# Row loads, spread rows, a lane for lambda and a split last store in a two-layer encoder

## The chip, the cores and the metric

The kernel runs on one core of one Trainium2 chip. The metric is the device time of one execution in microseconds, as the median of several runs. A core has five engines that take their instructions in order, each from its own queue: TensorE (PE, matrix products), VectorE (DVE), ScalarE (ACT), GpSimd (POOL) and SyncE (SP, which here issues nearly all DMAs). They wait for each other by semaphores. SBUF is the on-chip memory of 128 partitions, PSUM the banks that TensorE writes.

## The reference

Two layers of a bidirectional encoder on 256 tokens of width 2048. A layer norm opens it; each layer projects to six parts, runs a diagonal state space model on two of them and a difference of two softmax maps on four, projects back, and normalises again.

```python
x = layer_norm(x, ln_emb_g, ln_emb_b)
for l in range(DEPTH):
    proj = jnp.einsum('bsd,de->bse', x, w_in[l])
    u, g_ssm, q, k, v, g_attn = jnp.split(proj, PROJ_SPLITS, axis=-1)
    ...
    lam = (jnp.exp(jnp.sum(lambda_q1[l].astype(f32) * lambda_k1[l].astype(f32)))
           - jnp.exp(jnp.sum(lambda_q2[l].astype(f32) * lambda_k2[l].astype(f32)))
           + lambda_init)
    o = diff_attention(qh, kh, vh, lam)
    o = rms_norm(o, attn_norm_g[l]) * (1.0 - lambda_init)
    ...
    out = jnp.einsum('bse,ed->bsd', mix, w_out[l])
    x = layer_norm(DEEPNORM_ALPHA * x + out, ln_g[l], ln_b[l])
```

`layer_norm` takes mean and variance over the 2048 columns of a token, and then multiplies by a row g and adds a row b, the same for all tokens.

## The kernel before

**Weights.** They stream in as jobs of 512 KB. SP loads each into one of four `raw` buffers (L150). ScalarE rounds it to `wh` (L163), VectorE takes the rest `wl` = raw - wh (L165), and a product is three matmuls: wh with xh, wh with xl, wl with xh (L169 to L171). The activations are split in the same way into `xh` and `xl`. So TensorE can't go on without a cast on ScalarE and a subtraction on VectorE for each job.

**The layer norm.** x lies in the tile `H` as two blocks of 128 tokens. `ln_stats` (L202) takes the statistics of 256 columns, `bn_aggr` (L222) joins them, GpSimd adds eps (L224) and takes the power -1/2 (L225), giving `rstd`. Then for each piece of up to 512 columns VectorE runs a centre row (L230: minus mean, times g) and a scale row (L236: times rstd, plus b). TensorE transposes the result (L249), ScalarE copies it to `xh` (L253), VectorE makes `xl` (L254). Each finished piece is also stored to `xres` (L211, one DMA a piece, issued by SP from a lane). Behind the second layer the pieces go to `out` instead (L241): for the second block in `LAST_PIECES` of (6,5,5) tiles of 128 columns, with two stores a piece, one for each half of 64 partitions.

**g and b.** `load_gb` (L198, L199) loads a part of the row into all 128 partitions; 512 columns are 256 KB of DMA. Ahead of layer 0 four such pairs stand on SP between the loads of x, the first part of the constants `cst` (L800), the first raws and the rest of the constants (L806, called cst2 below).

**Lambda.** `lam_of` (L653 to L666) loads four rows `on`, multiplies them (L655), reduces (L657), takes the exponent `le`, joins them to `nlam` (L663), loads `gsc` (L665) and scales it (L666). It is called at the start of each layer. gsc has two buffers, so the one of layer 1 is loaded in the head already.

**Tables.** `ssm_tables` makes the state space tables on VectorE from `kx`, scaled by `p_st` = exp(`p_ls`) (L303 to L312, on through L350); TensorE transposes them (`tp`, L375).

**What sets the order.** The side work is written as generators in lanes, which are called between the matmul groups; what they issue goes to a scheduler that orders each engine's queue when the kernel is built. DMA issues use semaphores in turn, so an issue on SP also waits for the landing of the DMA that stands eight places ahead of it.

Of the kernel before, what the change touches and what calls it, by code (L numbers as in the profile page):

```python
# [21 lines left out]
EPS = 1e-5  # L22
# [6 lines left out]

C_ID, C_SEL, C_EYE, C_MF, C_MB, C_COS, C_SIN, C_HP, C_W = 0, 128, 192, 208, 209, 210, 466, 722, 723  # L30

LAST_PIECES = (6,5,5)
RAW_BUFS = 4
SPLIT_AHEAD = 2
BUDGET = 1.6
# [1 line left out]
STORE_HOP = 2  # L37
LOAD_HOP = 10
SCAN_COST = 1.0
HEAD_HOPS = (1,1,2,2,2,3)  # L40


@with_exitstack
def kernel(
# [29 lines left out]
    mult, add, sub = ALU.mult, ALU.add, ALU.subtract  # L74
# [140 lines left out]
    def ln_finish(r, gt, bt, st, dst, box, ahead):  # L215
# [4 lines left out]
        def moments(i):  # L220
            mv = T([128, 2], "mv", 2)
            V.bn_aggr(mv, st[:, i].rearrange("p c s -> p (c s)"))  # L222
            rstd = T([128, 1], "rstd", 2)
            GP.tensor_scalar(rstd, mv[:, 1:2], EPS, None, add)  # L224
            pool[0] = GP.tensor_tensor(rstd, rstd, mhalf[:, 0:1], ALU.pow).ins  # L225
            return mv, rstd

# [4 lines left out]
        def norm(i, k0, nk, mv, rstd):  # L232
            cs = slice(k0 * 128, (k0 + nk) * 128)
            if dst is None or i == 0:
                centre(i, k0, nk, mv)
            last = V.scalar_tensor_tensor(r[:, i, cs], r[:, i, cs], rstd, bt[:, cs], mult, add)  # L236
            if dst is None:
                stores.append((xres[128 * i:128 * i + 128, cs], r[:, i, cs]))
            else:
                for j in range(2):  # L240
                    SY.dma_start(dst[2 * i + j][:, cs], r[64 * j:64 * j + 64, i, cs])  # L241
            return last.ins

        def trans(k0, nk, i0, ni):
# [402 lines left out]

    swap = list(range(8, 16)) + list(range(0, 8)) + list(range(16, 32))

    def lam_of(l):  # L650
        t = T([128, 4, 64], "on")
        for i, src in enumerate((lambda_q1, lambda_k1, lambda_q2, lambda_k2)):
            SY.dma_start(t[:, i, :], src[l:l + 1, :].to_broadcast([128, 64]))  # L653
        tv = t.rearrange("p (m k) d -> p m k d", m=2)
        V.tensor_tensor(tv[:, :, 0, :], tv[:, :, 0, :], tv[:, :, 1, :], mult)  # L655
        s2 = T([128, 2], "ls2", 2)
        V.tensor_reduce(s2, tv[:, :, 0, :], AX.X, add)  # L657
        e2 = T([128, 2], "le2", 2)
        A.activation(e2, s2, AF.Exp)
        neg = T([128, 1], "nlam", 2)  # L660
        init = 0.8 - 0.6 * math.exp(-0.3 * l)

        V.scalar_tensor_tensor(neg, e2[:, 1:2], -init, e2[:, 0:1], add, sub)  # L663
        gs = T([128, 1], "gsc", 2)
        SY.dma_start(gs, attn_norm_g[l].unsqueeze(1))  # L665
        V.tensor_scalar(gs, gs, 1.0 - init, None, mult)  # L666
        return neg, gs

    def rotary(ps, scale):
        qs = T([128, 2, 256], "qs")  # L670
# [120 lines left out]


    r, gt, bt = ln_tiles()
    for i in range(2):
        for c in range(2):
            cs = slice(1024 * c, 1024 * c + 1024)
            for j in range(2):
                SY.dma_start(r[64 * j:64 * j + 64, i, cs], xv[2 * i + j][:, cs])
        if i == 0:
            SY.dma_start(cst[:, 0:C_SEL], consts[:, 0:C_SEL])  # L800
            load_gb(gt, bt, ln_emb_g, ln_emb_b, slice(0, 512))
    for c in range(RAW_BUFS):
        load(c)
        if c < 3:
            load_gb(gt, bt, ln_emb_g, ln_emb_b, slice(512 * c + 512, 512 * c + 1024))
    SY.dma_start(cst[:, C_SEL:], consts[:, C_SEL:])  # L806
    st = T([128, 2, 8, 6], "st")
    box = {}
# [48 lines left out]
    for l in range(DEPTH):  # L857
# [17 lines left out]
            z.ublocks = b + 1  # L875

        l_store = Lane(store_x(), 1.5)
        neg, gsc = lam_of(l)
        hi, lo = X.hi, X.lo
        acc2 = [acc_bank(), acc_bank()]  # L880
        for s in range(4):
# [15 lines left out]
        for hp in range(4):  # L897
# [11 lines left out]
            A.copy(v, acc)  # L909
            finish(rk)  # L910
            if hp == 0:
                l_out = Lane(ssm_out(l), 4, after=[l_scan])
            every += [Lane(head(hp, h, store["q"], store["k"], v, oT, neg, gsc), 1 + 0.1 * h) for h in range(2)]
            heads = every[-2:]
        for b in range(4):
            acc = block(hi, lo)
# [153 lines left out]
```

## Time and profile before

| | us |
|---|---|
| median of 3 runs | 1031.38 (1029.9 to 1032.72) |
| the profiled execution | 1032.34 |
| its span on the core | 1030.6 |
| TensorE busy | 965.9 |
| VectorE busy | 773.8 |
| ScalarE busy | 605.9 |
| GpSimd busy | 67.7 |

The granted clock of TensorE is 0.985 of full speed in the mean over the span. The span is divided here into a head (0 to 60 us: layer norm of x, first jobs, tables), layer 0, the switch between the layers (around 524 to 550), layer 1, and the tail (from 1010, behind the last matmul).

### The profile page before, as it was taken

Reading aid. Unit: us, or ns where it says so; the run is one execution under the profiler, and the core shown is the slowest. Engines: PE = TensorE matmul, PEld = TensorE weight load, DVE = VectorE, ACT = ScalarE, POOL = GpSimd, SP = SyncE. Lnnn points to the kernel's source line nnn. Section 1 sums busy time; section 2 is a strip of 40 time slices with the busy share of each in tenths; the row PEclk is TensorE's granted clock in tenths of the full one; section 3 lists DMA queues with packets and bytes.
Section 4 is the critical chain, followed back from the end, with each engine's and each line's share of the span. In section 5 each row is a group of like instructions: output and inputs, shape, how many; then the busy total and the mean of one; then the engine's idle time right before and its main releaser. Section 6 shows DMA issues by size and latency. Waiting matters only on the chain.

```text
span 1030.6 us, 23623 instructions
## 1 busy us (share of the span) xinstructions
PE 965.9 (94%) x9792; PEld 932.7 (91%) x9792; DVE 773.8 (75%) x1310; ACT 605.9 (59%) x962; POOL 67.7 (7%) x104
## 2 busy tenths in 40 slices
PE   2899999999999988999889999999999998999995
PEld 2889988999999887999879989999999897999995
DVE  6875799899887666655588699988988566565676
ACT  2546586655575899444344585565566879843640
POOL 1000131010010000000010120010010000000001
PEclk9999999999999998999999999999999999999998
DMA  9897522455465524779965724545455443677973
GB/s 270 240 271 218 179 62 62 146 182 165 144 193 164 174 88 124 247 241 303 275 207 166 232 59 146 177 152 162 152 162 179 142 144 104 179 231 238 316 241 85
DMA packets 201867, 186.08 MB, mean 181 GB/s; under 512 B 38048, under 2 KB 194464, under 8 KB 201760
## 3 DMA queue, kind: packets, MB, share of 16 engines
q1 hardware_dynamic: 201760, 184.57, 58.4%
q8 instruction: 77, 1.26, 0.5%
q14 instruction: 30, 0.25, 0.1%
HBM read 169.21 MB, written 15.34 MB: 179 GB/s over the span
## 4 chain that ended last, share of the span: by engine, by line
PE 66%; ACT 11%; DMA 9%; DVE 7%; issue 3%; SPq 3%; POOL 1%; POOLq 0%; DVEq 0%; ACTq 0%
PE acc L169 19%; PE acc L170 18%; PE acc L171 18%; DMA raw<-in_w_out_dram 3%; ACT bh L630 3%; DVE wl L165 2%; ACT bh L629 2%; DMA rpart<-xr 2%; ACT wh L163 2%; PE ss L502 2%; PE sc L699 1%; PE tp L474 1%; PE ss L727 1%; PE ss L592 1%; DVE H L236 1%
## 5 line engine op out<-in xcount | busy, mean ns | idle before, releaser
L165 DVE TENSOR_TENSOR wl<-raw,wh 128x1024 fp32r<-128x1024 f32 x266 | 324.7, 1222 | 182.2 <-ACT wh L163 181.2
L163 ACT CAST wh<-raw 128x1024 fp32r<-128x1024 f32 x266 | 278.3, 1049 | 257.7 <-PE acc L170 109.6
L169 PE MATMUL acc<-xh,wh 128*128 128x256 f32 x1280 | 371.4, 291 | 2.4 <-ACT wh L163 1.3
L170 PE MATMUL acc<-xl,wh 128*128 128x256 f32 x1280 | 366.5, 286 | 3.0 <-DVE xl L254 2.9
L171 PE MATMUL acc<-xh,wl 128*128 128x256 f32 x1280 | 365.8, 286 | 1.8 <-DVE wl L165 1.8
L169 PEld LDWEIGHTS acc<-xh,wh 128*128 128x128 f32 x1280 | 246.3, 193 | 7.3 <-ACT xh L253 1.6
L170 PEld LDWEIGHTS acc<-xl,wh 128*128 128x128 f32 x1280 | 246.8, 193 | 4.9 <-DVE xl L254 4.0
L171 PEld LDWEIGHTS acc<-xh,wl 128*128 128x128 f32 x1280 | 246.7, 193 | 3.4 <-DVE wl L165 2.5
L169 PE MATMUL acc<-wh,xh 128*128 128x256 f32 x720 | 206.6, 287 | 2.7 <-ACT wh L163 1.9
L170 PE MATMUL acc<-wl,xh 128*128 128x256 f32 x720 | 205.7, 286 | 3.0 <-DVE wl L165 2.8
L171 PE MATMUL acc<-wh,xl 128*128 128x256 f32 x720 | 204.7, 285 | 0.0
L170 PEld LDWEIGHTS acc<-wl,xh 128*128 128x128 f32 x720 | 139.2, 193 | 4.1 <-DVE wl L165 4.0
L169 PEld LDWEIGHTS acc<-wh,xh 128*128 128x128 f32 x720 | 139.1, 193 | 3.7 <-ACT wh L163 2.5
L171 PEld LDWEIGHTS acc<-wh,xl 128*128 128x128 f32 x720 | 139.1, 193 | 0.1
L552 DVE TENSOR_TENSOR sa<-tab,H 128x256 f32<-128x256 f32 x126 | 53.1, 421 | 2.9 <-ACT H L505 0.7
L459 DVE TENSOR_TENSOR w<-w,x 128x512 f32<-128x512 f32 x64 | 45.5, 712 | 0.8
L709 ACT ACTIVATE e<-sc,mx 128x256 f32<-128x256 f32 x64 | 29.5, 476 | 19.3 <-DVE mx L703 19.3
L592 PE MATMUL ss<-bh,w 128*64 128x64 f32 x512 | 32.6, 236 | 6.5 <-ACT ub L599 6.5
L555 DVE TENSOR_TENSOR H<-sa 128x128 f32<-128x128 f32 x126 | 36.2, 287 | 2.1
L554 DVE TENSOR_TENSOR sa<-sa,H 128x128 f32<-128x128 f32 x126 | 36.1, 286 | 1.9
L505 ACT COPY H<-ss 128x512 f32<-128x512 f32 x32 | 33.9, 1176 | 4.1 <-PE ss L502 4.1
L171 PE MATMUL acc<-bh,wl 128*128 128x256 f32 x128 | 36.1, 282 | 0.0
(189 smaller groups left out, 1292.9 us busy)
## 6 DMA issues: line engine op xcount, KB each, us to landing
raw<-in_w_in_dram SPq DMA_DIRECT2D x192, 512.0 KB, 3.5
raw<-in_w_out_dram SPq DMA_DIRECT2D x64, 512.0 KB, 5.4
raw<-in_w_glu_dram SPq DMA_DIRECT2D x16, 512.0 KB, 5.4
xr<-xres SPq DMA_DIRECT2D x16, 256.0 KB, 3.5
rpart<-xr SPq DMA_DIRECT2D x16, 256.0 KB, 5.1
xr<-rpart SPq DMA_DIRECT2D x15, 256.0 KB, 4.6
xres<-H SPq DMA_DIRECT2D x14, 256.0 KB, 3.7
H<-in_x_dram SPq DMA_DIRECT2D x8, 256.0 KB, 5.9
```

The lines of the kernel that those rows point to most:

```text
L163: A.copy(wh, raw)
L165: V.tensor_tensor(wl, raw, wh.bitcast(F32), sub)
L169: PE.matmul(o, lhsT=lh, rhs=rh, start=first, stop=False, skip_group_check=True)
L170: PE.matmul(o, lhsT=lh, rhs=rl, start=False, stop=False, skip_group_check=True)
L171: PE.matmul(o, lhsT=ll, rhs=rh, start=False, stop=last, skip_group_check=True)
L459: V.tensor_tensor(w[:, r], w[:, r], x2, op)
L505: A.copy(z.H[:, 2 * o:2 * o + 2, 1:65].rearrange("p q k r g -> p q (r g) k")[:, :, g2::2], ps[g2].rearrange("p q r g k -> p q (r g) k"))
L552: V.tensor_tensor(a.rearrange("p v q r g -> p v q (r g)"), lam, h.unsqueeze(1).to_broadcast([128, 2, 16, 8]), mult)
L554: V.tensor_tensor(a[:, 0], a[:, 0], nx, add)
L555: V.tensor_tensor(nx, a[:, 0], a[:, 1, :, ::-1, :], add)
L592: PE.matmul(dst, lhsT=w[:, ri, g].rearrange("p c j -> p (c j)"), rhs=hc[:, g // 4, ri, g % 4, :], start=ri == 0, stop=False, skip_group_ch ...
L630: A.copy(hc[64:128], src[64:128, :, :, ::-1])
```

## The change

It has four parts.

1. SP loads g and b as two rows of 1x2048 ahead of x, then all of x with the first constants between its halves, then four raws, then the rest of the constants. A matmul of `ones` (1x128) with 512 columns of a row spreads it over the 128 partitions of PSUM, and ScalarE copies it to SBUF: eight matmuls, eight copies. These use the `acc` banks, of which there are two.
2. In the moments the add of eps is on VectorE; the power stays on GpSimd.
3. `lam_of` is a lane. It is finished ahead of the first attention heads at the latest; its gsc load stands next to the loads of `on`.
4. `LAST_PIECES` is (6,5,3,2), and of the two stores of each piece SP issues one and ScalarE the other.

```diff
-LAST_PIECES = (6,5,5)
+LAST_PIECES = (6,5,3,2)
...
+LAM_HOP = 4
...
-            GP.tensor_scalar(rstd, mv[:, 1:2], EPS, None, add)
+            V.tensor_scalar(rstd, mv[:, 1:2], EPS, None, add)
             pool[0] = GP.tensor_tensor(rstd, rstd, mhalf[:, 0:1], ALU.pow).ins
...
-                for j in range(2):
-                    SY.dma_start(dst[2 * i + j][:, cs], r[64 * j:64 * j + 64, i, cs])
+                for j, eng in enumerate((SY, A)):
+                    eng.dma_start(dst[2 * i + j][:, cs], r[64 * j:64 * j + 64, i, cs])
...
-    def lam_of(l):
+    def lam_of(l, out):
+        yield 0.0, LAM_HOP
         t = T([128, 4, 64], "on")
         for i, src in enumerate((lambda_q1, lambda_k1, lambda_q2, lambda_k2)):
             SY.dma_start(t[:, i, :], src[l:l + 1, :].to_broadcast([128, 64]))
+        gs = T([128, 1], "gsc", 2)
+        SY.dma_start(gs, attn_norm_g[l].unsqueeze(1))
+        yield 0.0, LAM_HOP
...
-        gs = T([128, 1], "gsc", 2)
-        SY.dma_start(gs, attn_norm_g[l].unsqueeze(1))
         V.tensor_scalar(gs, gs, 1.0 - init, None, mult)
-        return neg, gs
+        out["neg"], out["gsc"] = neg, gs
+        yield 0.6, 0
...
+    rows = [T([1, 2048], tag) for tag in ("bh", "c8")]
+    ones = T([1, 128], "kw")
+    GP.memset(ones, 1.0)
+    for row, src in zip(rows, (ln_emb_g, ln_emb_b)):
+        SY.dma_start(row, src.unsqueeze(0))
...
-            load_gb(gt, bt, ln_emb_g, ln_emb_b, slice(0, 512))
     for c in range(RAW_BUFS):
         load(c)
-        if c < 3:
-            load_gb(gt, bt, ln_emb_g, ln_emb_b, slice(512 * c + 512, 512 * c + 1024))
+    for c in range(4):
+        cs = slice(512 * c, 512 * c + 512)
+        for row, full in zip(rows, (gt, bt)):
+            t = PS([128, 512], "acc", 2)
+            PE.matmul(t, lhsT=ones, rhs=row[:, cs], start=True, stop=True)
+            A.copy(full[:, cs], t)
...
-        neg, gsc = lam_of(l)
+        lam = {}
+        l_lam = Lane(lam_of(l, lam), 1.2)
...
             if hp == 0:
+                finish(l_lam)
```

Since a scheduler sets the order, the diff alone does not tell what stands where. In the rows below a row is line, operation, and output<-input with a shape; x4 is four of the same.

SP, the small loads of the head. Before, the p_ls loads, the first xres stores and the second gsc:

```order
L306 DMA p_ls<-in_ssm_log_step_dram 64x1 x2
L211 DMA xres<-H 128x512
L211 DMA xres<-H 128x256 x2
L211 DMA xres<-H 128x512 x4
L436 DMA dd<-in_ssm_d_dram 16x16x1 x3
L150 DMA raw<-in_w_in_dram 128x4x256
L436 DMA dd<-in_ssm_d_dram 16x16x1
L211 DMA xres<-H 128x512
L945 DMA bg<-in_b_glu_dram 128x8x1
L665 DMA gsc<-in_attn_norm_g_dram 128x1
```

With the change, SP from the last two p_ls loads on (the raw is the fifth), as far as the first gsc:

```order
L307 DMA p_ls<-in_ssm_log_step_dram 64x1 x2
L151 DMA raw<-in_w_in_dram 128x4x256
L212 DMA xres<-H 128x512
L212 DMA xres<-H 128x256
L655 DMA on<-in_lambda_q_dram 128x64
L151 DMA raw<-in_w_in_dram 128x4x256
L655 DMA on<-in_lambda_k_dram 128x64
L151 DMA raw<-in_w_in_dram 128x4x256
L655 DMA on<-in_lambda_q_dram 128x64
L655 DMA on<-in_lambda_k_dram 128x64
L657 DMA gsc<-in_attn_norm_g_dram 128x1
```

and directly behind these, as far as the second gsc:

```order
L212 DMA xres<-H 128x256
L437 DMA dd<-in_ssm_d_dram 16x16x1
L212 DMA xres<-H 128x512
L437 DMA dd<-in_ssm_d_dram 16x16x1 x2
L212 DMA xres<-H 128x512
L437 DMA dd<-in_ssm_d_dram 16x16x1
L959 DMA bg<-in_b_glu_dram 128x8x1
L212 DMA xres<-H 128x512
L657 DMA gsc<-in_attn_norm_g_dram 128x1
```

The loads of on stood far ahead, behind cst2; they now stand behind p_ls and among raws five to seven. The second gsc stands behind the sixth xres store instead of the eighth.

VectorE in the head. Before, from the product of the lambda rows (on) to the fourth wl; the xl rows are those of x's tiles 4 and 5, then 6 and 7:

```order
L655 TENSOR_TENSOR on<-on 128x2x64
L254 TENSOR_TENSOR xl_119<-ss,xh_118 128x512
L236 SCALAR_TENSOR_TENSOR H<-H,rstd 128x512
L230 SCALAR_TENSOR_TENSOR H<-H,mv 128x512
L666 TENSOR_SCALAR gsc<-gsc 128x1
L657 TENSOR_REDUCE ls_177<-on 128x2
L165 TENSOR_TENSOR wl<-raw,wh 128x1024
L254 TENSOR_TENSOR xl_119<-ss,xh_118 128x512
```

With the change, from the reduction of the same rows (their product, the first gsc, a scale and a centre stand right ahead) to the same wl and xl:

```order
L662 TENSOR_REDUCE ls_622<-on 128x2
L237 SCALAR_TENSOR_TENSOR H<-H,rstd 128x512
L231 SCALAR_TENSOR_TENSOR H<-H,mv 128x512
L320 SCALAR_TENSOR_TENSOR kx<-kx 128x128
L668 SCALAR_TENSOR_TENSOR nlam<-le_624 128x1
L669 TENSOR_SCALAR gsc<-gsc 128x1
L237 SCALAR_TENSOR_TENSOR H<-H,rstd 128x512
L231 SCALAR_TENSOR_TENSOR H<-H,mv 128x512
L320 SCALAR_TENSOR_TENSOR kx<-kx 128x128
L166 TENSOR_TENSOR wl<-raw,wh 128x1024
L255 TENSOR_TENSOR xl_141<-ss,xh_140 128x512 x2
```

The second gsc row (L669 here, in before far behind the fourth wl) now stands ahead of the fourth wl and of both xl.

VectorE at the start of layer 1. Before, around the xl of the second block's tiles 4 to 7:

```order
L230 SCALAR_TENSOR_TENSOR H<-H,mv 128x512
L254 TENSOR_TENSOR xl_6540<-ss,xh_6539 128x4x128
L236 SCALAR_TENSOR_TENSOR H<-H,rstd 128x512
L230 SCALAR_TENSOR_TENSOR H<-H,mv 128x512
L165 TENSOR_TENSOR wl<-raw,wh 128x1024
L236 SCALAR_TENSOR_TENSOR H<-H,rstd 128x512
```

With the change, from the same centre row on (tab,bh are products for the state space tables):

```order
L231 SCALAR_TENSOR_TENSOR H<-H,mv 128x512
L237 SCALAR_TENSOR_TENSOR H<-H,rstd 128x512
L231 SCALAR_TENSOR_TENSOR H<-H,mv 128x512
L237 SCALAR_TENSOR_TENSOR H<-H,rstd 128x512
L458 TENSOR_TENSOR x_7165<-tab,bh 128x512
L458 TENSOR_TENSOR w_7164<-tab,bh 128x512
L458 TENSOR_TENSOR w_7216<-tab,bh 128x512
L255 TENSOR_TENSOR xl_6562<-ss,xh_6561 128x4x128
L458 TENSOR_TENSOR w_7216<-tab,bh 128x512
L166 TENSOR_TENSOR wl<-raw,wh 128x1024
```

The xl and the wl behind it moved past the last scale and centre rows and past three products. On TensorE, the 32 table transposes of the head (`tp`, L375) stand between matmuls in 18 runs before (12 single, 2 pairs, 4 of four) and in 11 with the change (2 single, 3 pairs, 6 of four).

## Rows read from the trace of the kernel before

**Rows 1.** The page, part 1: busy time of each engine.

```profile
PE 965.9 (94%) x9792; PEld 932.7 (91%) x9792; DVE 773.8 (75%) x1310; ACT 605.9 (59%) x962; POOL 67.7 (7%) x104
```

**Rows 2.** The chain of waits in the head: start us, length us, what.

```profile
6.63 8.45 DMA H<-in_x_dram
...
58.36 0.20 PE tp L375
58.56 0.32 PE acc L169
58.88 0.12 PE acc L170
...
72.03 0.26 PE tp L375 x2
```

**Rows 3.** VectorE in the head: start, length, line, operation; in brackets idle time before.

```profile
11.16 0.75 DVE L236 SCALAR_TENSOR_TENSOR H<-H,rstd 128x512 f32<-128x512 f32 x1 [0.94 <-DMA H<-in_ln_emb_b_dram]
...
18.74 0.48 DVE L236 SCALAR_TENSOR_TENSOR H<-H,rstd 128x256 f32<-128x256 f32 x1 [0.77 <-POOL rstd L225]
...
28.64 0.29 DVE L655 TENSOR_TENSOR on<-on 128x128 f32<-128x128 f32 x1
28.84 0.68 DVE L254 TENSOR_TENSOR xl<-ss,xh 128x512 fp32r<-128x512 f32 x1
...
45.15 0.15 DVE L666 TENSOR_SCALAR gsc<-gsc 128x1 f32<-128x1 f32 x1 [4.54 <-DMA gsc<-in_attn_norm_g_dram]
```

**Rows 4.** Stretches: length, busy us (PE, PEld, DVE, ACT, POOL), clock, DMA share, GB/s.

```profile
15.00:20.00 5.00, 0.69 (x2) 0.29 (x2) 4.02 (x9) 1.04 (x1) 1.08 (x2) 1.00 1.07 396
...
40.00:45.00 5.00, 4.12 (x35) 3.92 (x34) 0.62 (x2) 1.78 (x3) 0.00 (x0) 1.00 0.97 247
45.00:50.00 5.00, 3.98 (x31) 3.78 (x32) 4.78 (x11) 3.25 (x5) 0.00 (x0) 1.00 0.93 254
50.00:60.00 10.00, 9.81 (x80) 9.41 (x79) 9.90 (x30) 5.07 (x6) 0.00 (x0) 1.00 0.81 255
```

**Rows 5.** DMA issues of the first 50 us: count, KB each, us to landing.

```profile
raw<-in_w_in_dram SPq DMA_DIRECT2D x13, 512.0 KB, 5.5
...
kx<-in_ssm_lam_re_dram SPq DMA_DIRECT2D x2, 32.0 KB, 3.0
...
p_ls<-in_ssm_log_step_dram SPq DMA_DIRECT2D x4, 0.2 KB, 3.2
```

**Rows 6.** VectorE at the start of layer 1.

```profile
536.22 0.59 DVE L236 SCALAR_TENSOR_TENSOR H<-H,rstd 128x256 f32<-128x256 f32 x1 [0.47 <-POOL rstd L225]
...
544.80 0.69 DVE L254 TENSOR_TENSOR xl<-ss,xh 128x512 fp32r<-128x512 f32 x1 [1.35 <-ACT xh L253]
...
546.73 1.22 DVE L165 TENSOR_TENSOR wl<-raw,wh 128x1024 fp32r<-128x1024 f32 x1
```

**Rows 7.** VectorE in the tail.

```profile
1012.99 0.76 DVE L236 SCALAR_TENSOR_TENSOR H<-H,rstd 128x512 f32<-128x512 f32 x1 [0.76 <-POOL rstd L225]
...
1020.27 1.81 DVE L230 SCALAR_TENSOR_TENSOR H<-H,mv 128x768 f32<-128x768 f32 x2
1022.55 1.02 DVE L236 SCALAR_TENSOR_TENSOR H<-H,rstd 128x768 f32<-128x768 f32 x1 [0.47 <-POOL rstd L225]
```

**Rows 8.** SP's queue in the head: start, length of the issues, line, what.

```profile
31.79 5.21 SPq L211 DMA_DIRECT2D xres<-H  x7
...
40.63 0.87 SPq L665 DMA_DIRECT2D gsc<-in_attn_norm_g_dram  x1
```

**Rows 9.** TensorE, the first matmul with the xl of tiles 4 and 5.

```profile
30.74 0.28 PE L170 MATMUL acc<-xl,wh 128*128 128x256 f32 x1
```

**Rows 10.** SP's queue in the tail: the last two issues.

```profile
1026.39 1.18 SPq L241 DMA_DIRECT2D out_dram<-H  x2
```

**Rows 11.** DMA issues of the tail: count, KB each, us to landing.

```profile
out_dram<-H SPq DMA_DIRECT2D x8, 128.0 KB, 2.3
out_dram<-H SPq DMA_DIRECT2D x4, 160.0 KB, 2.5
```

More of the change, by code (lines that the diff above doesn't have):

```diff
@@ L911 @@
             if hp == 0:
+                finish(l_lam)
                 l_out = Lane(ssm_out(l), 4, after=[l_scan])
-            every += [Lane(head(hp, h, store["q"], store["k"], v, oT, neg, gsc), 1 + 0.1 * h) for h in range(2)]
+            every += [Lane(head(hp, h, store["q"], store["k"], v, oT, lam["neg"], lam["gsc"]), 1 + 0.1 * h) for h in range(2)]
             heads = every[-2:]
```

## The prediction

> **What bounds the kernel now.** I read the page first, then the table by stretches, then the chain of waits, and last the queues row by row at the three places that the change touches. TensorE is busy 94% of the span [rows 1], so a microsecond counts only where TensorE waits for others: in the first 60 us, at the switch between the layers, and in the tail behind the last matmul. In the head the chain goes back to the last piece of x, which lands at 15.08 (6.63 + 8.45) [rows 2]. Later in the head VectorE stands still for 4.54 us for the second load of gsc [rows 3]; in the two stretches around it TensorE is busy 4.12 and 3.98 of 5 us, so 1.90 us are lost there, and from 50 us on it is busy 9.81 of 10 [rows 4]. A step at 30 us is therefore paid for unless it fills a hole that is there anyway.
>
> The profiled execution took 1032.34 us for a span of 1030.6; the median of the runs is 0.96 us below it. I make the sum against 1032.34 and take off 0.96. What can be told from no change here is about 0.3%, 3.1 us.
>
> **The head.** *x.* Two row loads of 8 KB stand ahead of x: two issues of up to 0.6 us, taken as +0.9. The first g and b pieces (512 KB) no longer lie ahead of x's second half: at the 250 GB/s or so of the stretches from 40 [rows 4] that is 2.1 us. Last x: 15.08 + 0.9 - 2.1 = 13.9. Eight one-row matmuls and eight copies spread g and b. By the transposes' 0.065 us per 64 columns [rows 2] a matmul of 512 columns takes 0.5 us, three times that at worst; TensorE and ScalarE are busy 0.69 and 1.04 of the 5 us from 15 to 20 [rows 4], so this is covered and costs nothing, and without that cover up to 4 us.
>
> *p_ls.* On SP the four p_ls loads now stand behind the four raws and cst2, and an issue waits for the landing of the DMA eight places ahead, which for the fourth p_ls is cst2. Four raws of 524 KB and 305 KB after 13.9: at the 396 GB/s of the stretch from 15 to 20 [rows 4] 6.1 us, at 250 9.6, so cst2 lands at 20.0 to 23.5. I take 20.3, since the stretch at 396 is of the same loads. The p_ls then lands 3.2 us later [rows 5], at 23.5, and p_st is there at 23.8. VectorE reaches the kx rows that want it at about 22.7 (second norm at 16.5, three wl of 1.1, which is 1.22 less their overlap [rows 6], norms and xl) and waits 1.1 us. On ScalarE the eighth copy queues behind p_st, which holds the second accumulator's bank until about 24.4; nothing hangs on that, as the next step is later.
>
> *on.* Behind p_st VectorE works through kx, scale, centre and xl, some 4.1 us at 0.66 per 512 columns (1.81 for 1408 [rows 7]), and at 27.9 wants the four lambda rows. Eight places ahead of the fourth of them is the fifth raw, issued at 20.9; a raw takes 5.5 here [rows 5], so the issue is at 26.4 and the landing 3.0 to 3.5 later [rows 5], at 29.6. Bounds: 28 and 31.
>
> *gsc.* Then on (0.20 [rows 3]), two scale-centre pairs and small rows, 3.7 us, and at 33.3 VectorE wants the second gsc. Its DMA stands behind the sixth xres store, which waits for a scale that ends at 30.6; with store and issue (seven stores take 5.21 [rows 8]) it goes out at 31.1 to 32.5, and lands 4.5 later, as it did in before: the same load was issued at 40.63 and used at 45.15 [rows 3, 8]. That is 35.6 to 37.0; I take 36.1. So this stall is not removed by the lane; it moves forward, to a place where the fourth wl and the xl of x's tiles 4 to 7 stand behind it. After it: scale, centre, kx (1.6), wl 1.1, xl 0.6: the first xl is there at 39.6, where it was started at 28.84 in before and TensorE used it at 30.74 [rows 3, 9]. TensorE's third batch starts 8.9 us late.
>
> *What is given back.* Before loses 1.90 us at 40 to 50 to its own gsc stall [rows 4], which the new order no longer has there. The 32 transposes of the tables stood in 18 runs and now stand in 11. One alone costs 0.20 and makes the next matmul 0.32 instead of 0.12, 0.40 in all; the second of a pair adds only 0.06 [rows 2]. A broken run so costs 0.34, seven fewer give 2.4, in a stretch where TensorE is full. Head: 8.9 - 1.9 - 2.4 = **+4.6**, bounds +1.4 (small loads of 2.3 us, below) to +7 (cst2 at 23.5, less what it overlaps with the later waits).
>
> **The layer switch.** The add of eps goes from GpSimd to VectorE. VectorE waits 0.47 for GpSimd at the second norm [rows 6] and as long or longer at the first; the new row costs about 0.14 there. One product (0.55) now runs ahead of it, so the second norm begins about 0.7 sooner. But the xl of the tiles 4 to 7, which ran at 544.80 after 1.35 idle [rows 6], now stands behind three more scale and centre rows (2.0) and three products of tab and bh (1.6), and the third job's wl, at 546.73 [rows 6], behind that xl and one product. Stepped from the centre that precedes them: 542.0 + 2.6 + 1.6 + 0.6 + 0.55 + 1.1 = 548.5, where that wl ended at 547.9: **+0.7**. Bounds: -0.7 (TensorE doesn't ask that early) and +1.9 (the products at 0.63 and the last store ahead of the raw).
>
> **The tail.** The 0.76 us wait at the first norm [rows 7] shrinks to 0.1, as only the power stays on GpSimd. VectorE then runs through to the last moments, where it waited 0.47 after two centres [rows 7]; the power now ends under those centres. The rows after that hold 2688 columns in before and after, with two more starts. VectorE ends about 0.8 sooner. The last piece has two stores, one on each queue: of the two issues that end the fourteen in before (1.18 [rows 10]) one is saved, 0.59. It is 64 KB a store, not 160: landing takes 2.5 us at 160 KB and 2.3 at 128 [rows 11], so about 0.4 less. Sum **-1.8**, bounds -1.0 (both queues held up by one another) and -2.3.
>
> On two issuing engines, the Trainium skill ("DMA: Bandwidth & Descriptors", section "Issuing engines are not separate DMA queues") says that both run on the same 16 DMA engines and that only the time to initiate is saved. By that the halves gain one issue and no bandwidth, the same 0.59; had they gained bandwidth as well, the tail would be nearer -2.3.
>
> **The middle** keeps its work, in an order that differs by a row here and there, on a full TensorE: 0, give or take 1.
>
> Sum: 4.6 + 0.7 - 1.8 = +3.5; 1032.34 + 3.5 - 0.96 = **1034.9, said as 1035.0**.
>
> **Rivals.** *Small loads land fast.* If the on and gsc loads take 2.3 us, as the stores of the tail do [rows 11], on is there at 28.7 and gsc at 33.0 (issued at 30.7); the first xl ends at 36.4, 3.2 us sooner: 1031.7, no change. For it: fewer raws stand between them. Against: 3.0 to 4.5 in the head of before [rows 3, 5]. It decides if the wait on gsc is under 1 us. The Trainium skill ("DMA: Bandwidth & Descriptors", section "Anatomy of one DMA", told of the path that GpSimd issues) gives about 2.0 us of fixed cost; by that the time would be 1031.1, but the trace of the head does not agree, at 3.2 for 0.2 KB.
>
> *VectorE's time counts, not TensorE's* (the faster side). VectorE is busy 9.90 of 10 us from 50 to 60 [rows 4]. If it, and not TensorE, sets the head's length, what counts is its idle time: after 1.1 + 1.7 + 2.8 = 5.6, before 4.54 + 0.77 + 0.94 [rows 3] = 6.25. The head is then -0.6, the switch -0.7 (its rows are only exchanged), the tail -1.8: 1031.38 - 3.1 = 1028.3. Against: TensorE is busy 9.81 of the same 10 us, and each xl that is late stops it at once.
>
> *Raws come late.* The eighth raw now stands behind the seventh xres store and the second gsc on SP. If ScalarE then waits for raws at 45 to 60, where TensorE has nothing in stock, the 1.9 us given back and some 1.5 more are lost: 1038.3.
>
> **How the numbers follow.** Forecast 0.50, from 1032.9 to 1037.5 by its bounds: 0.32 of it above 1034.5, 0.18 within 0.3%. Small loads fast 0.18, within. VectorE counts 0.19: 0.15 under 1028.3, 0.04 within. Raws late 0.13, slower. Slower 0.45, same 0.40, faster 0.15. The range from 1028.5 to 1039 leaves out about 0.1 on either side.
>
> **What would show it.** Right: VectorE waits for p_ls, on and gsc one after the other between 22 and 37 us, the xl of tiles 4 to 7 runs near 39, TensorE has a hole of 6 us or more ahead of it and none of note from 45 to 50; rstd waits on GpSimd of 0.1 us; last stores issued by two engines at the same moment. Wrong: gsc landed before VectorE asks; the xl before 34; a matmul count at 100 us that is no later than before; or waits of ScalarE for raws between 45 and 60.

## The result: 1.3% slower, and the profile after

| | before | after |
|---|---|---|
| median of 6 runs, us | 1032.28 (1029.9 to 1035.94) | 1045.69 (1041.59 to 1048.49) |
| after / before, 95% interval | | 1.0127 (1.010 to 1.0153) |
| the profiled execution, us | 1032.34 | 1045.82 |
| its span, us | 1030.6 | 1044.0 |

The same two kernels were run once more among the experiments: 1034.14 and 1042.06, a ratio of 1.0088 (1.0056 to 1.0119). So the change costs 9 to 13 us. The forecast was +3.5 us, the range ended at 1039: the sign was right, the size was not, and the time lies outside the range.

Part 1 of the page of after, the busy time of each engine, beside [rows 1]:

```profile
PE 986.6 (94%) x9808; PEld 944.1 (90%) x9808; DVE 774.0 (74%) x1318; ACT 609.0 (58%) x970; POOL 68.8 (7%) x99
```

VectorE does the same work as before to 0.2 us. TensorE has only 16 instructions more, the eight spreads with two each, and yet 20.7 us more of busy time: 13.7 for the spreads (eight of 1.71, below). The other 7.0 are near what the 68 more slow matmuls counted below would cost (68 x 0.093 = 6.3).

**Where the wait is.** The table of waits on TensorE, 20 to 60 us, after: what was waited for, us in total, times, longest:

```profile
PE acc L170 <- ACT xh L254: 4.2, 1, 4.2
PE acc L171 <- DVE xl L255: 3.2, 1, 3.2
```

Two engines, not one, are late. VectorE in the same stretch (start, length, line, operation, in brackets the idle time before it), beside [rows 3]:

```profile
22.89 0.24 DVE L312 TENSOR_SCALAR kx<-kx,p_st 128x64 f32<-128x64 f32 x1
...
32.47 0.29 DVE L660 TENSOR_TENSOR on<-on 128x128 f32<-128x128 f32 x1 [5.40 <-DMA on<-in_lambda_k_dram]
...
34.27 0.28 DVE L662 TENSOR_REDUCE ls<-on 128x2 f32<-128x128 f32 x1
...
36.80 0.15 DVE L669 TENSOR_SCALAR gsc<-gsc 128x1 f32<-128x1 f32 x1 [0.66 <-DMA gsc<-in_attn_norm_g_dram]
...
38.40 1.22 DVE L166 TENSOR_TENSOR wl<-raw,wh 128x1024 fp32r<-128x1024 f32 x1
39.53 0.68 DVE L255 TENSOR_TENSOR xl<-ss,xh 128x512 fp32r<-128x512 f32 x1
```

kx does not wait for p_st; the row that stops the engine is the product of the lambda rows. ScalarE:

```profile
34.58 0.20 ACT L664 ACTIVATE le<-ls 128x2 f32<-128x2 f32 x1 [10.64 <-DVE ls L662]
34.69 1.03 ACT L164 CAST wh<-raw 128x1024 fp32r<-128x1024 f32 x1
35.63 1.06 ACT L254 CAST xh<-ss 128x512 fp32r<-128x512 f32 x2
```

`le`, the exponent of the lambda sums, stands ahead of the fourth cast and of the xh of x's tiles 4 to 7. It can't run before `ls`, and `ls` not before `on` has landed. Not all of the 10.64 us are lost: `wh` has three buffers, and the fourth cast can't start before TensorE is through with the first of them, at about 29.8. (In o_after, below, it starts at 29.35, right behind the same matmul.) So for some 4.9 us a row of 0.20 holds up a cast that could run. TensorE then, beside [rows 9] (its first matmul with the new xl, 30.74 in before):

```profile
36.26 0.80 PE L170 MATMUL acc<-xh,wh 128*128 128x256 f32 x2 [4.21 <-ACT xh L254]
40.27 0.58 PE L171 MATMUL acc<-xl,wh 128*128 128x256 f32 x1 [3.22 <-DVE xl L255]
...
41.51 0.41 PE L170 MATMUL acc<-xh,wh 128*128 128x256 f32 x1
41.72 0.41 PE L171 MATMUL acc<-xl,wh 128*128 128x256 f32 x1
```

Two holes, 4.21 and 3.22. Behind them 20 matmuls run slowly, 0.213 us from one to the next, and the ones from 45.7 on 0.12 apart. The stretches of one microsecond show why (length, busy us of PE, PEld, DVE, ACT, POOL, granted clock, DMA share, GB/s):

```profile
34.00:35.00 1.00, 0.00 (x0) 0.00 (x0) 1.00 (x4) 0.42 (x2) 0.00 (x0) 1.00 0.56 22
35.00:36.00 1.00, 0.00 (x0) 0.00 (x0) 1.00 (x4) 1.00 (x2) 0.00 (x0) 0.65 0.86 247
36.00:37.00 1.00, 0.74 (x2) 0.50 (x2) 0.34 (x4) 1.00 (x3) 0.00 (x0) 0.50 0.50 24
...
45.00:46.00 1.00, 1.00 (x8) 1.00 (x8) 1.00 (x5) 0.00 (x0) 0.00 (x0) 0.73 1.04 368
```

The granted clock falls from full (2.4 GHz) to half (1.2 GHz) at about 35.4, in the first hole, and comes back at about 45.5. The 20 matmuls lose 20 x 0.093 = 1.9 us, and the four transposes among them some 0.35 (0.70 where the next four take 0.36): these two holes cost more than their length.

**Where the difference piles up.** Start of the n-th cast `wh` of a weight block on ScalarE, in us. The third column is an experiment told below (p_tail), whose program has the order of before up to the last piece:

| cast | before | p_tail | after | after again |
|---|---|---|---|---|
| 36th (head over) | 170.33 | 168.94 | 177.18 | 177.50 |
| 48th (layer 0, heads) | 208.20 | 206.81 | 216.50 | 216.02 |
| 96th (layer 0, end) | 379.06 | 377.73 | 389.84 | 387.55 |
| 216th (layer 1) | 824.51 | 825.20 | 837.12 | 837.15 |
| 264th | 990.30 | 994.74 | 1006.26 | 1007.28 |
| span | 1030.6 | 1033.0 | 1044.0 | 1044.8 |

Against before's profile the head is +6.9, against p_tail's +8.2. The execution of before that was profiled was 1.4 slower than p_tail's in the head, and 3.8 faster between the 216th and the 264th cast, where all other kernels that were profiled lost 1.8 to 7.9 on it. So the 3.4 us that seem to be lost there most likely belong to that one execution of before. p_tail is the fairer partner: head +8.2, heads +1.5, end of layer 0 +2.4, then -0.6 to the 264th cast and -0.5 to the end, 11.0 in all.

### The profile page after: what moved, and what is told of

The parts are those of the page before. It is cut to its first block, busy times and chain, and to the rows that moved or that the text cites. A ratio compares the mean times of both kernels' runs of the same rounds, so it can differ in the third digit from the quotient of the medians.

```text
span 1044.0 us, 23670 instructions
## 1 busy us (share of the span) xinstructions
PE 986.6 (94%) x9808; PEld 944.1 (90%) x9808; DVE 774.0 (74%) x1318; ACT 609.0 (58%) x970; POOL 68.8 (7%) x99
## 3 DMA queue, kind: packets, MB, share of 16 engines
q8 instruction: 77, 1.26, 0.5%
## 4 chain that ended last, share of the span: by engine, by line
PE 36%; DMA 10%; ACT 10%; DVE 6%; issue 2%; SPq 1%; POOL 0%; DVEq 0%; ACTq 0%
PE acc L170 10%; PE acc L171 10%; PE acc L172 10%; DMA rpart<-xr 4%; DMA raw<-in_w_out_dram 4%; ACT bh L631 3%; ACT bh L630 2%; DVE wl L166 2%; ACT wh L164 2%; DMA raw<-in_w_glu_dram 1%; PE ss L503 1%; DVE H L237 1%; PE tp L475 1%; DVE H L231 1%; PE ss L593 1%
## 5 line engine op out<-in xcount | busy, mean ns | idle before, releaser
L170 PEld LDWEIGHTS acc<-xh,wh 128*128 128x128 f32 x1280 | 249.7, 196 | 13.8 <-ACT xh L254 5.3
L171 PEld LDWEIGHTS acc<-xl,wh 128*128 128x128 f32 x1280 | 249.9, 195 | 5.0 <-DVE xl L255 4.2
L172 PEld LDWEIGHTS acc<-xh,wl 128*128 128x128 f32 x1280 | 249.8, 195 | 2.9 <-DVE wl L166 2.1
```

The lines of the kernel that those rows point to most:

```text
L170: PE.matmul(o, lhsT=lh, rhs=rh, start=first, stop=False, skip_group_check=True)
L171: PE.matmul(o, lhsT=lh, rhs=rl, start=False, stop=False, skip_group_check=True)
L172: PE.matmul(o, lhsT=ll, rhs=rh, start=False, stop=last, skip_group_check=True)
```

## Experiments

Times are medians against the kernel before on the same chip (1034.11, 1034.62 and 1034.14 in the three groups), ratios with their 95% intervals.

### One part alone: the rows, the lane, the last pieces

p_rows is before with the rows part only (x in one go, g and b spread by TensorE):

```diff
+    rows = [T([1, 2048], tag) for tag in ("bh", "c8")]
...
-            load_gb(gt, bt, ln_emb_g, ln_emb_b, slice(0, 512))
...
+            PE.matmul(t, lhsT=ones, rhs=row[:, cs], start=True, stop=True)
+            A.copy(full[:, cs], t)
```

> The kernel before with the first part of the change alone: g and b as rows ahead of x, spread by TensorE and ScalarE; lambda at the start of the layer, eps on GpSimd, old tail. In this order the rows wl of the fourth job and xl of x's tiles 4 to 7 stand on VectorE behind the second gsc, as in the changed kernel, but the loads of on are issued right behind cst2, and the exponent le, which stands on ScalarE ahead of the fourth wh, no longer has to wait for them. Theory (late small loads hold ScalarE and VectorE, and TensorE then runs at its lower clock): a hole of TensorE from 32 us that ends near 37 instead of 40, some 20 matmuls at half speed behind it, +4 to +7 us against before. Rival (the lambda lane is the whole cause): within 1.5 us of before. Rival (the spread itself, matmuls and copies, is the cause): +10 or more.

Measured: 1042.18, 1.0073 (1.0047 to 1.0098): 8.1 us, a little over the theory's range. p_lam is before with the lambda lane only:

```diff
-        neg, gsc = lam_of(l)
+        lam = {}
+        l_lam = Lane(lam_of(l, lam), 1.2)
```

> The kernel before with the lambda lane alone. Its order keeps the fourth wl and the xl of tiles 4 to 7 ahead of on, gsc and le on their engines, so the late on loads have nothing of the first jobs behind them. Theory (position behind a late load): no hole at 32 to 40, -2 to +2 us against before. Rival (the lane is the cause by itself): +4 or more. Rival (the lane's second gsc still stops VectorE as in before): the stall of 4.5 us stays and the time is that of before.

Measured: 1033.98, 1.000 (0.9977 to 1.0024), as the theory said. p_tail is before with the last pieces and the two issuing engines only:

```diff
-LAST_PIECES = (6,5,5)
+LAST_PIECES = (6,5,3,2)
...
+                for j, eng in enumerate((SY, A)):
+                    eng.dma_start(dst[2 * i + j][:, cs], r[64 * j:64 * j + 64, i, cs])
```

> The kernel before with the last part alone: pieces of 6, 5, 3, 2 and the stores from SP and ScalarE. The trace of the changed kernel has the last stores issued at the same moment and landing 2.7 us later, so a smaller store lands no sooner: one issue less and a smaller last piece give -0.5 to -1.2 us in the trace from the last add to the last landing; the median moves by as much, if the rest of the order is as before. Rival (the rest of the kernel is put in another order by the scheduler): a difference ahead of 1010 us that is larger than that.

Measured: 1034.9, 1.0006 (0.9977 to 1.0035). The rows alone make most of the loss; lane and tail, each alone, can't be told from nothing. In p_rows the order is another than in after, and the loss much the same. Its hole was expected to end near 37 and ended at 39.23, for another small load was late than the one in mind. Its ScalarE, and then its TensorE:

```profile
30.32 0.20 ACT L308 ACTIVATE p_st<-p_ls 128x2 f32<-128x2 f32 x1 [4.92 <-DMA p_ls<-in_ssm_log_step_dram]
```

```profile
39.23 0.58 PE L170 MATMUL acc<-xl,wh 128*128 128x256 f32 x1 [5.77 <-DVE xl L254]
```

Here p_ls is the late load and p_st the row ahead of the fourth cast, which starts at 31.39. Which small load it is changes; that a row on a small load stands ahead of cast and xl doesn't.

### The change without one part: the lane, the rows; and eps alone

n_lam is the change with `lam_of` as in before (the lane's diff above, taken back).

> The changed kernel without the lambda lane (rows, eps on VectorE, new tail). Theory (late on loads behind p_ls hold ScalarE's le and with it the fourth wh): the hole ends near 37, 3 us sooner than with the lane, and the time is 4 to 8 us under the changed kernel. Rival (the second gsc and the order on VectorE decide, whatever the on loads do): within 2 us of the changed kernel. Rival (eps on VectorE is what reorders the middle): the 6 us that the changed kernel loses behind 120 us stay.

Measured: 1044.03, 1.0093 (1.0057 to 1.0129), so the theory failed and the rival's time came: ScalarE waits 5.81 ahead of p_st and casts the fourth block at 31.59, VectorE waits 4.56 for p_st, and TensorE's hole ends at 39.41. As in p_rows, p_ls has taken the place of on. n_rows is the change with the loads of g, b and x as in before (p_rows's diff taken back).

> The changed kernel without the row loads and the spread (g and b by broadcast loads, as before; lane, eps on VectorE and new tail stay). Theory (the rows part is the cause, by the order that it brings): in this order on, gsc and nlam stand behind the fourth wl and the xl on VectorE, no load holds the first jobs, within 3 us of before. Rival (the parts add up, with eps and lane as large as the rows): 4 us or more above before.

Measured: 1040.79, 1.0071 (1.0044 to 1.0099). That was not expected, and p_eps gives a reason: before, with the add of eps on VectorE and nothing else.

```diff
-            GP.tensor_scalar(rstd, mv[:, 1:2], EPS, None, add)
+            V.tensor_scalar(rstd, mv[:, 1:2], EPS, None, add)
```

> The kernel before with the add of eps on VectorE alone. Theory: it saves 0.5 us at each of the two norms of the switch and 0.5 at each of the two of the tail, as the trace of the changed kernel shows, but the scheduler reorders the head too: the on product, gsc and two more norm pairs now stand ahead of the fourth wl and the xl; -1 to +3 us. Rival (the move is a plain gain): -1.5 or less.

Measured: 1039.91, 1.0049 (1.0021 to 1.0076), more than the theory's 3 us. Six instructions of 0.15 us, moved to another engine, cost 5 us. VectorE of p_eps (on stands at 27.05), and its TensorE (before's on is at 28.64 and its first xl at 28.84 [rows 3]):

```profile
32.69 1.28 DVE L254 TENSOR_TENSOR xl<-ss,xh 128x512 fp32r<-128x512 f32 x2
...
43.72 0.15 DVE L666 TENSOR_SCALAR gsc<-gsc 128x1 f32<-128x1 f32 x1 [5.12 <-DMA gsc<-in_attn_norm_g_dram]
```

```profile
33.43 0.39 PE L170 MATMUL acc<-xl,wh 128*128 128x256 f32 x1 [2.04 <-DVE xl L254]
...
45.72 0.39 PE L171 MATMUL acc<-xh,wl 128*128 128x256 f32 x1 [3.42 <-DVE wl L165]
```

In the new order three more pairs of scale and centre stand ahead of the xl, and gsc ahead of a wl. (That the scheduler reckons with another time for the norm is argued, not shown.) So the parts do not add up: rows +8.1, eps +5.3, both with the tail (n_lam) +9.9. Each of the two spoils the order of the same stretch. p_eps also shows that a hole can come from the order of VectorE's rows alone: 2.04 us, where VectorE waits for no load ahead of the xl.

### The small loads early, on ScalarE's queue

If the late small loads are the cause, issuing them at the start should give the head back. f_after is the change and f_before the kernel before, both with

```diff
+    for l in range(2):
+        ps = slice(64 * l, 64 * l + 64)
+        for d in range(2):
+            A.dma_start(early["p_ls"][ps, d:d + 1], ssm_log_step[l, d].unsqueeze(1))
...
+    for l in range(DEPTH):
+        A.dma_start(early["gsc"][l], attn_norm_g[l].unsqueeze(1))
     r, gt, bt = ln_tiles()
```

and so with kx and on.

> The changed kernel, but the small loads of the head (p_ls, kx, on of layer 0, both gsc) are issued by ScalarE's queue at the very start, beside x, and so are in long before anyone asks. The norm rows stay ahead of the xl of x's tiles 4 to 7 on VectorE, and the row spread stays. Theory (a small load queued behind raws and stores is late, and what stands in order behind the one who waits for it is late with it): no wait on p_ls, on or gsc, the first xl of tiles 4 and 5 near 32 instead of 39.5, no hole of more than 2 us and no slow matmuls behind it; 6 to 10 us under the changed kernel, about the time of before. Rival (the order of the norm rows ahead of the xl makes the hole by itself): under 3 us gained. Rival (the spread matmuls keep TensorE): the start of the main matmuls, not the hole, is what is late, and it stays.

Measured: 1042.89, 1.008 (1.0053 to 1.0107).

> The kernel before with the same small loads issued by ScalarE at the start. Theory: before's own wait of 4.5 us for the second gsc goes, but the scheduler puts more norm rows ahead of the xl of tiles 4 to 7 and TensorE waits there instead: -2 to +2 us. Rival (every wait of VectorE in the head costs its length): -4 or less.

Measured: 1042.18, 1.007 (1.0035 to 1.0104). Nothing is won, and both theories failed. The statistics of x on VectorE, first in after, then in f_after:

```profile
13.21 1.41 DVE L203 BATCH_NORM_STATS2 st<-H 128x6 f32<-128x256 f32 x4 [0.23 <-DMA H<-in_x_dram]
```

```profile
18.32 1.40 DVE L203 BATCH_NORM_STATS2 st<-H 128x6 f32<-128x256 f32 x4 [4.97 <-DMA H<-in_x_dram]
```

The last piece of x comes 5.1 us later: it lands at 18.23 instead of 13.12. For 3.5 of these it is not yet issued (SP issues it at 9.88 instead of 6.34, when the first constants have landed at 9.87; these stand eight places ahead of it, since the loads on ScalarE's queue take places in the same turn of semaphores); then it takes 8.35 to land instead of 6.78. ScalarE's own start moves as well, since its queue is busy with issues, and so the first weight matmul:

```profile
16.89 1.28 ACT L825 ACT_TABLE_LOAD   x1 [16.89 <-DMA on<-in_lambda_q_dram]
```

```profile
32.79 0.56 PE L170 MATMUL acc<-xh,wh 128*128 128x256 f32 x1
```

It stands at 20.98 in after. From there to 46 the longest hole is 1.30; the loss sits at the start instead. The experiment moved the cost and so could not show the cause. It does show another thing: the second queue was not a free lane. The Trainium skill ("DMA: Bandwidth & Descriptors", section "Issuing engines are not separate DMA queues") says that DMAs of different issuing engines run on the same 16 DMA engines and interleave there. The longer landing of x's last piece, by 1.6 us, agrees with it.

### The same loads, their waiters moved: the test that decides

o_after leaves every load where the change has it and forces only the order: p_st on ScalarE behind the newest cast, the kx, on and gsc rows on VectorE behind the newest wl.

```diff
-        A.activation(step, ls, AF.Exp)
...
+        yield 0.0, 3
+        with after(last["wh"]):
+            A.activation(step, ls, AF.Exp)
+        with after(last["wl"]):
...
-        V.tensor_scalar(gs, gs, 1.0 - init, None, mult)
+        with after(last["wl"]):
+            V.tensor_scalar(gs, gs, 1.0 - init, None, mult)
```

> The changed kernel; every load is issued from the same engine and place, and as late. Only what waits for them is moved: p_st on ScalarE and the first kx rows on VectorE have to stand behind the casts and subtractions of the fifth and later jobs, and the product of on and the two gsc rows behind the newest wl. So ScalarE's fourth wh and VectorE's fourth wl and xl of tiles 4 to 7 have no small load ahead of them, but the norm rows stay ahead of them. Theory (the wait of small loads ahead of the first jobs): the first xl near 32 instead of 39.5, TensorE's hole of 8 us shrinks to about 1 and no slow matmuls follow it, so the stretch to 60 us is 7 to 9 us shorter; some of that is lost again where TensorE is full, and the whole is 5 to 8 us under the changed kernel. Rival (all the work that has to be done by 120 us is the limit, whatever its order, as it seemed with the loads on ScalarE's queue): under 2 us gained.

Measured: **1029.83**, 4.3 us less than before: 0.9956 (0.9929 to 0.9984), and 12.2 us less than the change in the same group, where 5 to 8 were expected. It is the fastest of all kernels here. VectorE and TensorE of o_after:

```profile
30.77 1.22 DVE L168 TENSOR_TENSOR wl<-raw,wh 128x1024 fp32r<-128x1024 f32 x1
31.91 1.28 DVE L257 TENSOR_TENSOR xl<-ss,xh 128x512 fp32r<-128x512 f32 x2
...
39.08 0.25 DVE L317 TENSOR_SCALAR kx<-kx,p_st 128x64 f32<-128x64 f32 x1
...
54.98 0.28 DVE L666 TENSOR_TENSOR on<-on 128x128 f32<-128x128 f32 x1
```

```profile
32.64 0.38 PE L173 MATMUL acc<-xl,wh 128*128 128x256 f32 x1 [0.89 <-DVE xl L257]
```

SP issues the second on_k load and the second gsc at 24.45 and 34.42, as in after (24.29 and 33.95). They land as late as they did, and no cast, wl or xl of these jobs stands behind their waiters: the hole is 0.89 instead of 4.21 and 3.22, the matmuls behind it are 0.12 apart, and the 36th cast starts at 167.16, 10.0 us before after's. The norm rows are still ahead of the xl, so they are not the cause of the long holes here. The loads were late in both; the loss in the head is what stood behind their waiters.

### Is it the clock? And is it VectorE's wait?

w_after is the change with 64 transposes of the identity on TensorE behind the second weight job, into a bank that nobody reads, to keep TensorE busy in the hole.

```diff
+        if ji == 2:
+            with after(newest_mm[0]):
+                t = tp_bank([128, 4, 128])
+                for n in range(64):
+                    PE.transpose(t[:, n % 4, :], ident, ident)
```

> The changed kernel with 64 transposes of the identity (7 us at full speed, into a bank that nobody reads) on TensorE between the second and the third job, where its hole is. Theory (a part of the hole's price is the clock: after it 20 matmuls ran 0.213 apart instead of 0.12): the hole is filled, the 20 matmuls run at full speed, and the stretch to 60 us is 1.5 to 2 us shorter than in the changed kernel. Rival (the matmuls behind the hole are slow because VectorE feeds them): they stay 0.21 apart and nothing is gained.

Measured: 1044.92, 1.0112 (1.0096 to 1.0129). The waits on VectorE are longer in this order (on 5.93, gsc 1.84), so the xl comes later still, and the transposes were done too early:

```profile
30.40 7.15 PE L844 MATMUL tp<-cst 128*128 128x128 f32 x64
37.31 0.36 PE L172 MATMUL acc<-xh,wh 128*128 128x256 f32 x1
41.76 0.39 PE L173 MATMUL acc<-xl,wh 128*128 128x256 f32 x1 [4.09 <-DVE xl L257]
```

```profile
42.00:43.00 1.00, 1.00 (x8) 1.00 (x8) 1.00 (x3) 0.00 (x0) 0.00 (x0) 0.71 0.69 172
43.00:44.00 1.00, 1.00 (x7) 1.00 (x7) 1.00 (x2) 0.84 (x3) 0.00 (x0) 0.50 1.00 347
```

The clock was at full through the hole of 4.09 and fell behind it, when the matmuls ran again, to 1.2 GHz until about 45.8: some 16 slow matmuls instead of 20. So the theory failed, and the clock's share can't be told from this total. Counted in after's trace, it is 1.9 us for the 20 matmuls.

g_before is before with both gsc in one DMA, so that the wait of 4.54 us on VectorE [rows 3] is gone.

```diff
-        gs = T([128, 1], "gsc", 2)
-        SY.dma_start(gs, attn_norm_g[l].unsqueeze(1))
+        if l == 0:
+            both["gsc"] = T([128, DEPTH], "gsc")
+            SY.dma_start(both["gsc"], attn_norm_g.rearrange("l p -> p l"))
+        gs = both["gsc"][:, l:l + 1]
```

> The kernel before with both gsc columns loaded by one DMA at the start of layer 0, so that no second gsc load stands behind the xres stores; the order around the first jobs stays. Theory (before's own wait of 4.5 us costs TensorE 1.9 us): the wait is gone and the stretch to 60 us is 1 to 2 us shorter than in before. Rival (VectorE's wait is made up for anyway): no difference at 120 us.

Measured: 1034.77, 1.0006 (0.9981 to 1.0032), as the rival said. VectorE doesn't wait for gsc any more, and TensorE has a hole a little later instead. ScalarE and TensorE of before, then of g_before:

```profile
46.58 1.05 ACT L163 CAST wh<-raw 128x1024 fp32r<-128x1024 f32 x1 [2.18 <-DMA raw<-in_w_in_dram]
45.96 0.39 PE L170 MATMUL acc<-xl,wh 128*128 128x256 f32 x1 [1.84 <-DVE xl L254]
```

```profile
46.59 1.05 ACT L163 CAST wh<-raw 128x1024 fp32r<-128x1024 f32 x1 [3.47 <-DMA raw<-in_w_in_dram]
51.36 0.39 PE L169 MATMUL acc<-xh,wh 128*128 128x256 f32 x1 [2.28 <-ACT ub L876]
```

In before an xl does stand right behind gsc, and TensorE waits 1.84 for it. But the next raw lands at 46.48 in before and at 46.49 in g_before, so ScalarE's cast of it starts at the same time in both, and what stands behind that cast (another cast, the copy of `ub`) is now what TensorE waits for. 4.5 us of VectorE's idle time were worth nothing here, because another late load lay just behind them.

a_again is the kernel after, unchanged.

> The changed kernel once more, for a second profile beside the others on the same chip. Theory (its loss in the head is of the program, the later ones are partly of the execution): the offset against before at 120 us is again 6 to 8 us; of the steps at 355, 830 and 960 us of the first profile at least one is not seen again. Rival (all of it is of the program): the same steps at the same places.

Measured: 1042.06, 1.0088 (1.0056 to 1.0119). Its casts stand in the table above. The head comes again to 0.3 us; the step at the end of layer 0 (+2.4) doesn't. After's hole of 1.91 at 357 is there in both executions (before: 1.32 and 0.76), but only in the first one some 15 slow matmuls follow it. So what is more in the first (1.5 to 2) belongs to an execution, not to the change.

## Why the prediction was right in sign and wrong in size

Two steps failed. In the head the hole on TensorE was priced by its length alone, and the matmuls at the lower clock behind it at nothing; they cost about 2.3 us. The middle of the kernel was put at 0, and came at 3.3 and 4.0 (36th to 264th cast, two executions of after against p_tail's). The waits that make the hole were forecast in the right place.

**The head, +4.6 forecast: the mechanism held, the term was too small by 2.3 against before's profile and by 3.6 against p_tail's.** x, cst2 and kx came within 1.1 us of the forecast, and p_ls 2.0 sooner (21.48 for 23.5). The chain's last link, the first xl of tiles 4 and 5 on TensorE, was forecast at 39.6 and came at 40.27. Two things were wrong on the way.

- *on*: forecast to land at 29.6; VectorE got it at 32.47. The step took 3.0 to 3.5 from [rows 5] (which has 3.0 and 3.2, for kx and p_ls) for loads that stand among raws. The fitting rows were in the trace of before and weren't taken: the loads of on themselves, 18 to 34 us (what, KB each, us to landing), first before, then after with gsc:

```profile
on<-in_lambda_q_dram SPq DMA_DIRECT2D x2, 32.0 KB, 7.2
on<-in_lambda_k_dram SPq DMA_DIRECT2D x2, 32.0 KB, 6.4
```

```profile
on<-in_lambda_q_dram SPq DMA_DIRECT2D x2, 32.0 KB, 6.2
on<-in_lambda_k_dram SPq DMA_DIRECT2D x2, 32.0 KB, 6.9
...
gsc<-in_attn_norm_g_dram SPq DMA_DIRECT2D x2, 0.5 KB, 2.8
```

  With 6.4 in place of 3.2 the same step gives 32.8, and 32.47 came; but the fourth load was issued at 24.29 and not at 26.4, and it took up to 8.2. *gsc*, forecast with 4.5, landed in 2.8, so its wait was 0.66 where 2.8 was forecast. The errors cancel: 1.1 + 1.7 + 2.8 = 5.6 us of waits on VectorE were forecast for p_st, on and gsc, and 0 + 5.40 + 0.66 = 6.06 came. That the sum held to 0.5 us is luck.
- *ScalarE*: the prediction followed VectorE's queue only. That le stands ahead of the fourth cast and the xh wasn't in it. It didn't add to the total, since the xl ended later still. The spreads were said to be covered. TensorE works without a break from 15.32 to the first weight matmul at 20.98 (20.43 in before), and two spreads of 2.07 are in that time: they take up what x, there 2 us sooner, could have gained. It doesn't show in the end, for o_after has the same spreads and is ahead of p_tail by the 36th cast.

The missing term is the clock behind the hole: about +2.3, priced at nothing, of which 1.9 is the 20 matmuls. The xl is 9.5 us late (40.27 against 30.74 [rows 9]), and with the clock and the first transpose of the tables the 141st weight matmul stands 12.3 late (43.36 in before, 55.65 in after). By the 480th (96.56 and 103.34) it is 6.8: 5.5 are given back, where 1.9 + 2.4 = 4.3 was forecast. Before's own hole behind gsc is 1.84 of that, as forecast; the other 3.7 fall where the transposes of the tables stand, for 2.4. The 1.4 by which p_tail is ahead of before in the head are 0.55 at the first weight matmul (19.87 and 20.43) and 0.84 in that hole (1.00 and 1.84).

**The middle, 0 give or take 1: failed.** Against p_tail it is +1.5 between the 36th and the 48th cast (the attention heads of layer 0) in one execution and +0.7 in the other. There TensorE waits for a tile on ScalarE that is also named `on` (an attention head's result): 0.40 and 0.51 in the first, 0.51 in the second; neither before nor p_tail has such a wait there. At the end of layer 0 the first execution has +2.4, which goes with the slow matmuls behind the hole at 357; the second has +0.6 there, and +2.1 from there to the 216th cast in layer 1, 1.5 of it across the switch, with no more slow matmuls in that stretch than p_tail. Nor does the change make more of these: of weight matmuls with a record of 0.40 us or longer there are 81 and 58 behind 60 us in the two executions of after, 47 in before, 70 in p_tail and 75 in o_after. Only in the head are there more (48 and 47, against 14 in before and 24 in p_tail). What makes up the rest of the middle stays open.

**The switch, +0.7: not to be told.** From the 135th to the 144th cast after loses between -0.4 (first execution against before) and +1.5 (second against p_tail). The xl of tiles 4 to 7 does stand behind the norm's rows and the products, and the order was read rightly:

```profile
558.02 0.68 DVE L255 TENSOR_TENSOR xl<-ss,xh 128x512 fp32r<-128x512 f32 x1
```

But TensorE, which asks for it, waits 0.24 only. The bound's reason, that TensorE doesn't ask that early, was the right one. (By its own terms the sum was 548.5 - 547.9 = 0.6.)

**The tail, -1.8: -1.1.** From the last add to the last landing it was 19.33 (1010.15 to 1029.48) and is 18.20 (1024.86 to 1043.06). The first norm in after, beside [rows 7]:

```profile
1027.44 0.75 DVE L237 SCALAR_TENSOR_TENSOR H<-H,rstd 128x512 f32<-128x512 f32 x1 [0.45 <-POOL rstd L226]
```

The 0.76 went to 0.45, not to 0.1: the power on GpSimd took 0.99 where it had taken 0.57. The two last stores go out together:

```profile
out_dram<-H SPq DMA_DIRECT2D x1, 64.0 KB, 2.5
out_dram<-H ACTq DMA_DIRECT2D x1, 64.0 KB, 2.7
```

That saves the issue of 0.59, as forecast; that 64 KB land 0.4 sooner than 160 [rows 11] was wrong. 1.1 us is less than a median can resolve. In p_tail the same stretch is 19.11, a gain of 0.2 where 0.5 to 1.2 was expected: the two queues save some 0.5 behind VectorE's last row, and VectorE, with two more starts, ends 0.25 later. So most of after's 1.1 comes with eps on VectorE and not with the stores.

**The rivals.** *Small loads land fast* fell: 5.40 for on. *VectorE's time counts* fell: VectorE's waits in the head came to 6.06, for 6.25 in before, and the head is 6.9 longer; in g_before it idles 4.5 us less and nothing is won. *Raws come late* didn't happen in after: ScalarE doesn't wait for a raw between 45 and 60. That the order could be mended at no cost to the change (o_after) was not among them.

**What stays open.** What the head would be without the slow matmuls; why eps alone moves the scheduler so far; and where o_after gets the last of its 4.3 us. Its head is 1.8 less than p_tail's and its tail 0.9 shorter than before's, which leaves 1.6. Its profile doesn't show them: that execution (1035.07) was the slowest of its ten, and lost 3.0 on p_tail's between the 36th and the 264th cast. So of o_after's gain over the change the rows of the head show 10.0 of the 12.2 us; the rest is in the medians alone.

## What to carry to other kernels

When a change moves a load, look for every engine that has a row on it, and for what is queued behind that row; a row of 0.2 us that waits for 0.5 KB can hold up a weight job. Ask for a long hole on TensorE what the matmuls behind it cost at the lower clock: 16 to 20 slow ones followed the holes of after and w_after in the head, some 15 the one of 1.91 in one execution of two. If a scheduler orders the queues, any edit can move rows far from where it was made: look where side work stands against the main chain, and pin it behind the main chain's newest step rather than load it earlier.

## What the runs showed of the hardware

- A load of 32 KB that is issued among 512 KB loads took 5.1 to 7.3 us to land in after and 5.6 to 7.6 in before; one of 0.5 KB issued when they were through, 2.8. The Trainium skill ("DMA: Bandwidth & Descriptors", section "Anatomy of one DMA", told of the path that GpSimd issues) gives about 2.0 us of fixed cost; these loads are issued by SP, and the second is 0.8 above it, the first 3 and more.
- A spread of a row over 128 partitions (one row times 128 ones, 512 columns, full f32) takes 1.71 us from one to the next, where the first weight matmuls of the same execution take 0.213 for 256: four times as long a column, and above the forecast's worst case of 1.5.

```profile
7.75 1.91 PE L816 MATMUL acc<-c,kw 1*128 1x512 f32 x2
9.45 1.91 PE L816 MATMUL acc<-bh,kw 1*128 1x512 f32 x2
```

- The granted clock fell in after's first hole, but in w_after only behind the hole, with the matmuls running again. And the first 26 weight matmuls of after (22.3 to 28.4) stand 0.213 apart, as at 1.2 GHz, while the row of their stretch shows a granted clock of 1.00 (before's first ones do the same from 21.5 on). In the head the spacing tells more than the clock's column:

```profile
20.00:30.00 10.00, 9.26 (x44) 7.86 (x43) 7.08 (x17) 1.26 (x4) 0.00 (x0) 1.00 0.78 209
```

```profile
23.62 0.41 PE L170 MATMUL acc<-xh,wh 128*128 128x256 f32 x1
23.84 0.41 PE L171 MATMUL acc<-xl,wh 128*128 128x256 f32 x1
```

- The power on GpSimd took 0.99 and 1.26 us in after's tail where it had taken 0.57 and 1.07 in before's. At the 0.57 VectorE stood still, at the 0.99 it ran a centre row beside it; that this is the reason is not shown.
